# Two transformer blocks on one core: longer runs of small matmuls, another beginning, and a last projection with tokens on the partitions

## The chip, the cores and the metric

The kernel runs on one core of a Trainium2 chip. Its time is the time on the device in microseconds (us). Each core has five engines with instruction lists of their own, worked off in order: TensorE (PE, matmuls into PSUM; PEld is its loading of the stationary operand), VectorE (DVE), ScalarE (ACT), GpSimd (POOL) and SyncE (SP, which here only issues transfers). A list waits where its next instruction needs something that another engine or a transfer has not yet delivered.

## The reference

512 tokens of width 1024 in float32 pass two layers of a first block and one layer of a second. Cut to what matters here:

```
for l in range(2):
    h = rmsnorm(x, attn_norm[l])
    z = h @ w_in[l]            # c_q c_kv k_rope g_q g_k g_v g_lr g_g r_q r_k r_v r_g
    y_a = mla_branch(...)      # softmax attention, 4 heads, low-rank q and kv
    y_b = gla_branch(g_q, g_k, g_v, g_lr, g_g, ...)   # 4 heads, dk 32, dv 64
    y_c = retention_branch(r_q, r_k, r_v, r_g, ...)   # 4 heads, dk 32, dv 64
    x = x + concat([y_a, y_b, y_c]) @ w_out[l]
    h = rmsnorm(x, ffn_norm[l])
    u = h @ ffn_w_up[l]
    x = x + (silu(causal_dwconv(u[..., :2816], ...)) * u[..., 2816:]) @ ffn_w_down[l]
x = rmsnorm(x, final_norm)
# second block: windowed attention, grouped-query attention, attention to a memory
merged = gate_a * (oa @ w_br_a) + gate_b * (ob @ w_br_b) + gate_m * (om @ w_br_m)
out = merged @ w_out
x = x + rms_norm(out, g_post)

# inside gla_branch, a chunk of 64 tokens:
A = einsum('bhik,bhjk,bhijk->bhij', qb, kb, exp(b_i - b_j) for j <= i)
out = A @ v + (q * exp(b)) @ state
# inside retention_branch: scores = (q @ k) * D;  out = scores @ v + q_dec @ R
```

## The kernel before

The class `Prog` issues everything through a framework that tracks what depends on what and sets the order of each engine's list. Activations lie feature-major: x is a tile of 128 partitions x 8 x 512 tokens (`self.x`). Every product with a weight matrix is done as three matmuls with operands split into a high and a low part (`mm3`, L444 to L446: high x high, low x high, high x low), called dense matmuls here. In the profile `ps` is a dense product with the features on PSUM's partitions, `pt` one with the tokens there. A group of weights is loaded by SP (`load`, L407, tile `wst`), its high part taken on ACT (`whi`, L424) and the low part on DVE (`wlo`, L425); up to three groups are staged and three are split at a time.

A dense product is a generator. The queue `Fill` holds such generators, and `self.f(us)` pulls about so many microseconds of dense matmuls from it into the list; the table `PACE` says how many are pulled at each place. So small matmuls of the attention parts and dense ones alternate on PE.

PSUM's eight banks are two tags: three for dense products (`bank`), five for all else (`mbank`).

- **Beginning** (`__init__`, `layer`, `kr_dense`): SP loads x0, the first weight group kr, x1 to x7, and then the groups gqk0 and gqk1 (first and second half of the 1024 features of 256 columns). ACT makes xh and the squares, DVE xl and the sum `acc`. `tsq` (L515) sums over the partitions by transposes, `rsqrt` (L496 to L500) is a chain of tiny DVE steps on `Rt`, and `rows` (L529) spreads the result over the partitions, which ACT copies as R (L539). kr (80 columns) and then gqk run on PE meanwhile; glr, gq, gk are those products times R, and `u` (L781) needs glr.
- **GLA** (`gla`): the causal scores of a chunk are made level by level; at each of eight levels (five of them with masks, MASKED) 16 to 64 matmuls `lv` (L858) of 32 rows fill four banks, one for each head, and DVE (masked copies, L871) or ACT copies them into gD and gA. `f(PACE["gla"])` stands after each quarter of a level (each t).
- **`mix_out`** (L912, for GLA with gA, for retention with rA, twice each in two layers, so four places): for each of four tiles of 128 tokens and each head, two matmuls `o`, one for each half of 64 tokens: the first half with 64 rows of A and v, the second with 128. For t > 0 a matmul with the state (L907) comes first.
- **Retention** (`ret`): per head one bank `rsc` of four matmuls (L968), a product with the decay (`rA`, DVE) and `f(PACE["ret2"])`. Before them `states` (L886) makes U and, on DVE, the states.
- **End** (`finish`): w_out of the second block in four groups of 256 columns, tokens in two halves of 256 moving columns; squares on ACT, sums on DVE, then `tsq`, `rsqrt`, `rows`, product, and the sum with x. Result (1024, 512), which the host transposes.

The functions that the change touches:

## Time and profile before

| | |
|---|---|
| time before, median of 3 runs | 1990.25 us (1987.42 to 1991.47) |
| the profiled execution's own time, and its span | 1990.08 us, 1988.3 us |
| mean granted clock of PE over the span | 0.993 of full speed |
| PE busy | 1954.8 us, 98% |
| DVE busy | 1239.2 us, 62% |
| ACT busy | 793.4 us, 40% |
| POOL busy | 140.7 us, 7% |
| instructions | 28658 |

The span is the profile's stretch from the first to the last instruction on the engines; 1.8 us of the time lie around it. Busy shares are averages over the span. In a row of the trace a matmul of 4-byte numbers may have two records (the loading and the passes split it), so counts of records (x16) are not counts of matmuls; "busy" of a group of records that overlap reaches from the first one's start to the last one's end. The time from the start of one row to the start of the next is what the list spends.

### The profile page before, as it was taken

What the parts mean: (1) busy time and instruction counts of PE and PEld (TensorE: products, weight loads), DVE (VectorE), ACT (ScalarE), POOL (GpSimd) and SP (SyncE); (2) the same over time, 40 slices, a digit from 0 to 9 for tenths busy, and PEclk for the clock granted to TensorE, in tenths of its full rate; (3) what the DMA queues carried; (4) which work ended last, traced back from release to release, by engine and by line L of the source; (5) the groups of instructions that cost most, each with busy time, mean ns of one, the idle gap of its engine ahead of it and who ended that gap; (6) DMA issues with size and microseconds to landing.
All of it is one profiled execution on the core that took longest, in us unless ns stands there. A gap on an engine that the chain in (4) does not pass through costs nothing.

```text
span 1988.3 us, 28658 instructions
## 1 busy us (share of the span) xinstructions
PE 1954.8 (98%) x11351; PEld 1620.4 (81%) x11351; DVE 1239.2 (62%) x2299; ACT 793.4 (40%) x1473; POOL 140.7 (7%) x172
## 2 busy tenths in 40 slices
PE   9999999999999999999999999999999999999997
PEld 7879888888888878888888888887888877788887
DVE  6666576646556666576656466845456787655454
ACT  5545243222224635443222224525354456543242
POOL 1000000000000100000000000021131330000000
PEclk9999999999999999999999999999999999999998
DMA  5221123232323321133232334432222221123331
GB/s 196 60 80 44 64 89 101 84 109 85 106 80 107 94 67 50 41 96 95 93 90 96 103 113 123 135 109 67 75 75 67 75 64 54 63 67 98 101 96 54
DMA packets 55189, 172.30 MB, mean 87 GB/s; under 512 B 6494, under 2 KB 10096, under 8 KB 55056
## 3 DMA queue, kind: packets, MB, share of 16 engines
q1 hardware_dynamic: 53152, 165.47, 26.6%
q0 software_dynamic: 1760, 4.87, 0.9%
q8 instruction: 89, 1.46, 0.3%
q14 instruction: 44, 0.36, 0.1%
q10 hardware_dynamic: 144, 0.14, 0.0%
HBM read 167.05 MB, written 2.10 MB: 85 GB/s over the span
## 4 chain that ended last, share of the span: by engine, by line
PE 91%; DVE 5%; ACT 3%; issue 1%; POOL 0%; DMA 0%; DVEq 0%; POOLq 0%; ACTq 0%
PE ps L444 24%; PE ps L446 23%; PE ps L445 23%; PE pt L444 3%; PE pt L445 3%; PE pt L446 3%; PE o L912 2%; DVE wlo L425 1%; PE o L1029 1%; PE s L1006 1%; PE aq L1347 1%; PE bo L1596 1%; PE bpq L1584 1%; PE rows L529 1%; PE lv L858 1%
## 5 line engine op out<-in xcount | busy, mean ns | idle before, releaser
L424 ACT ACTIVATE whi<-wst 128x1024 fp32r<-128x1024 f32 (+3 forms) x318 | 316.3, 995 | 700.3 <-PE ps L445 566.4
L425 DVE TENSOR_TENSOR wlo<-wst,whi 128x1024 fp32r<-128x1024 f32 (+3 forms) x318 | 367.4, 1155 | 315.9 <-ACT whi L424 315.4
L444 PE MATMUL ps<-xh,whi 128*128 128x512 f32 (+1 forms) x1408 | 556.8, 396 | 0.0
L445 PE MATMUL ps<-xl,whi 128*128 128x512 f32 (+1 forms) x1408 | 550.3, 391 | 0.6 <-DVE xl L490 0.6
L446 PE MATMUL ps<-xh,wlo 128*128 128x512 f32 (+1 forms) x1408 | 549.8, 391 | 0.1
L444 PEld LDWEIGHTS ps<-xh,whi 128*128 128x128 f32 (+1 forms) x1408 | 264.4, 188 | 61.1 <-issue 6.7
L446 PEld LDWEIGHTS ps<-xh,wlo 128*128 128x128 f32 (+1 forms) x1408 | 264.3, 188 | 57.1 <-DVE wlo L425 0.9
L445 PEld LDWEIGHTS ps<-xl,whi 128*128 128x128 f32 (+1 forms) x1408 | 264.6, 188 | 55.8 <-DVE xl L490 2.8
L444 PE MATMUL pt<-whi,xh 128*128 128x256 f32 x480 | 143.2, 299 | 1.5 <-ACT bz L1523 0.8
L445 PE MATMUL pt<-wlo,xh 128*128 128x256 f32 x480 | 137.6, 287 | 0.0
L445 PE MATMUL ps<-fl,whi 128*128 128x512 f32 x352 | 137.0, 389 | 0.0
L444 PE MATMUL ps<-fh,whi 128*128 128x512 f32 x352 | 137.0, 389 | 0.0
L446 PE MATMUL ps<-fh,wlo 128*128 128x512 f32 x352 | 136.9, 389 | 0.0
L446 PE MATMUL pt<-whi,xl 128*128 128x256 f32 x480 | 136.5, 286 | 0.0
L444 PEld LDWEIGHTS pt<-whi,xh 128*128 128x128 f32 x480 | 92.7, 194 | 6.7 <-ACT bz L1523 1.3
L1067 DVE TENSOR_TENSOR x<-x,ps 128x512 f32<-128x512 f32 x96 | 65.7, 687 | 50.8 <-PE ps L446 50.6
L445 PEld LDWEIGHTS pt<-wlo,xh 128*128 128x128 f32 x480 | 93.3, 194 | 0.5 <-issue 0.2
L446 PEld LDWEIGHTS pt<-whi,xl 128*128 128x128 f32 x480 | 92.9, 194 | 0.2 <-issue 0.2
L445 PEld LDWEIGHTS ps<-fl,whi 128*128 128x128 f32 x352 | 66.1, 188 | 13.8
L446 PEld LDWEIGHTS ps<-fh,wlo 128*128 128x128 f32 x352 | 66.1, 188 | 13.7
L444 PEld LDWEIGHTS ps<-fh,whi 128*128 128x128 f32 x352 | 66.1, 188 | 13.6
L486 ACT ACTIVATE fh<-cv 128x512 fp32r<-128x512 f32 x44 | 27.9, 633 | 84.7 <-DVE cv L1121 84.7
(464 smaller groups left out, 2919.1 us busy)
## 6 DMA issues: line engine op xcount, KB each, us to landing
wst<-in_w SPq DMA_DIRECT2D x250, 512.0 KB, 3.5
wst<-in_w SPq DMA_DIRECT2D x54, 384.0 KB, 3.0
wst<-in_w SPq DMA_DIRECT2D x20, 256.0 KB, 2.6
x<-in_xT SPq DMA_DIRECT2D x8, 256.0 KB, 4.9
out<-out SPq DMA_DIRECT2D x8, 256.0 KB, 2.3
mt<-in_memT POOLq DMA_DIRECT2D x4, 256.0 KB, 4.1
c<-in_cst POOLq DMA_DIRECT2D x3, 256.0 KB, 3.5
s<-in_cst POOLq DMA_DIRECT2D x3, 256.0 KB, 2.9
```

The costliest lines, as they stand in the source:

```text
L424: nc.scalar.activation(hi, s3, AF.Copy)
L425: nc.vector.tensor_sub(lo, s3, hi.bitcast(F32))
L444: nc.tensor.matmul(out, lh, rh, start=start, stop=False, skip_group_check=True)
L445: nc.tensor.matmul(out, lh, rl, start=False, stop=False, skip_group_check=True)
L446: nc.tensor.matmul(out, ll, rh, start=False, stop=stop, skip_group_check=True)
L486: nc.scalar.activation(hi, src, AF.Copy)
L529: nc.tensor.matmul(ps[:, t, :], w, self.ident, start=True, stop=True)
L858: nc.tensor.matmul(ps[h][j0:j0 + w, t, c0:c0 + w], ke[hp, a:a + w], qe[hp, a + off:a + off + w], start=True, stop=True, tile_position=(32 ...
L912: nc.tensor.matmul(o[r, j, hd], A[h][:n, t, r], v[t][:n, hd], start=t + h == 0, stop=True, skip_group_check=True)
L1006: nc.tensor.matmul(s[:, :nk], qn[h][:, T4[qt]], kn[h][:, :nk], start=False, stop=True, skip_group_check=True)
L1029: nc.tensor.matmul(O[qt][:, h, :], PT[u][:, T4[kt]], v[kt][:, T4[h]], start=kt == 0, stop=kt == qt)
L1067: nc.vector.tensor_add(xm, xm, ps)
```

## The change

Ten edits go together:

1. x0, x2, x4, x6 are issued by SP and x1, x3, x5, x7 by ACT; the first three weight groups stand on SP after x0, x2 and x4.
2. kr's weights are split in two halves into tiles of their own, and kr and gqk share each part of x: for each of the eight parts three matmuls for kr, then six for gqk.
3. The squares of layer 0's first norm are made by GpSimd; DVE adds them up.
4. In `gla` the dense work of a level is pulled once, after all 32 matmuls, in place of four times.
5. In `mix_out` the state matmuls of a pair of tiles come first, and all A times v have 128 rows.
6. In `ret` all four heads' scores stand in one run, the heads rotating, in four banks.
7. w_out of the second block comes as two groups of 512 columns.
8. `residual` transposes x to token-major (32 transposes, in place) while branch products are worked off.
9. `finish` has the tokens on the partitions: the token tile of x is the stationary operand, 512 columns move; sums of squares come from ACT's accumulator, each tile of 128 tokens has its own small `rsqrt`, and one fused DVE instruction scales and adds x.
10. g_post is loaded as an array of its own by GpSimd, and the result leaves as (512, 1024) in eight transfers, half issued by SP and half by ACT.

```
-    two("out", "w_out_2", k8, _span(0, 1024))
+    for i in range(2):
+        g.append(((2, "out", i), "w_out_2", 0, k8, _span(512 * i, 512)))
...
         for k in range(8):
-            nc.sync.dma_start(self.x[:, k], aps["xT"][128 * k:128 * k + 128])
-            if k == 0:
-                self.load(0)
-        self.load(2)
+            (nc.scalar if k % 2 else nc.sync).dma_start(self.x[:, k], aps["xT"][128 * k:128 * k + 128])
+            if k % 2 == 0:
+                self.load(min(k // 2, 2))
...
+        if i in (self.table[(0, "kr")][0], self.table[(1, "kr")][0]):
+            hi, lo = (TileList([self.gt(n, (128, 4, mc), F32R) for _ in range(2)], 4) for n in ("krwh", "krwl"))
+            for j in range(2):
+                self.split(hi.tiles[j], lo.tiles[j], s3[:, 4 * j:4 * j + 4])
+            self.wt[i] = (k, kt, hi, lo)
+            return
...
-    def sumsq(self, tiles, gain=None):
+    def sumsq(self, tiles, gain=None, pool=False):
         nc = self.nc
         acc = self.gt("acc")
+        if pool:
+            for i, s in enumerate(tiles):
+                q = self.gt("sq") if i else acc
+                nc.gpsimd.tensor_mul(q, s, s)
+                if i:
+                    nc.vector.tensor_add(acc, acc, q)
+            return acc
...
-        ps, pg = {}, {}
-        yield from self.dense((l, "kr"), self.xh, self.xl, 8, ps.__setitem__)
-        yield from self.dense((l, "gqk"), self.xh, self.xl, 8, pg.__setitem__)
+        ps, pg = [self.bank("ps")], [self.bank("ps") for _ in range(2)]
+        _, _, rh, rl = next(self.weights((l, "kr")))
+        for k0, kt, hi, lo in self.weights((l, "gqk")):
+            for k in range(kt):
+                x = self.xh[:, k0 + k], self.xl[:, k0 + k], k0 + k == 0, k0 + k == 7
+                sl = slice(0, 80)
+                self.mm3(ps[0][:80], rh[:, k0 + k, sl], rl[:, k0 + k, sl], *x)
+                yield 0.65
+                for m in range(2):
+                    sl = slice(128 * m, 128 * m + 128)
+                    self.mm3(pg[m], hi[:, k, sl], lo[:, k, sl], *x)
+                yield 1.3
         while self.R is None:
             yield 0.5
...
                         nc.tensor.matmul(ps[h][j0:j0 + w, t, c0:c0 + w], ke[hp, a:a + w], qe[hp, a + off:a + off + w],
                                          start=True, stop=True, tile_position=(32 * h, j0))
-                f(PACE["gla"])
+            f(4 * PACE["gla"])
...
+            first = True
             for j in range(2):
                 t = 2 * tp + j
-                sl = slice(t * 128, t * 128 + 128)
                 if t:
-                    nc.tensor.matmul(o[:, j], qg[:, sl], st[t], start=j == 0, stop=True, skip_group_check=True)
+                    nc.tensor.matmul(o[:, j], qg[:, t * 128:t * 128 + 128], st[t], start=first, stop=True,
+                                     skip_group_check=True)
+                    first = False
+            for j in range(2):
+                t = 2 * tp + j
                 for h in range(4):
                     hd = slice(64 * h, 64 * h + 64)
-                    for n in (64, 128):
-                        r = slice(n - 64, n)
-                        nc.tensor.matmul(o[r, j, hd], A[h][:n, t, r], v[t][:n, hd], start=t + h == 0, stop=True,
+                    for r in (slice(0, 64), slice(64, 128)):
+                        nc.tensor.matmul(o[r, j, hd], A[h][:, t, r], v[t][:, hd], start=False, stop=True,
                                          skip_group_check=True)
...
+        ps = [self.mbank("rsc", (128, 4, 128)) for _ in range(4)]
+        for t in range(4):
+            for h in range(4):
+                hp = slice(32 * h, 32 * h + 32)
+                nc.tensor.matmul(ps[h][:, t, :], rk[hp, T4[t]], rq[hp, T4[t]], start=True, stop=True)
         for h in range(4):
-            hp = slice(32 * h, 32 * h + 32)
-            ps = self.mbank("rsc", (128, 4, 128))
-            for t in range(4):
-                nc.tensor.matmul(ps[:, t, :], rk[hp, T4[t]], rq[hp, T4[t]], start=True, stop=True)
             a = self.gt("rA", (128, 4, 128))
-            nc.vector.tensor_mul(a, ps, rd[:, h:h + 1, :].to_broadcast([128, 4, 128]))
+            nc.vector.tensor_mul(a, ps[h], rd[:, h:h + 1, :].to_broadcast([128, 4, 128]))
             A.append(a)
-            f(PACE["ret2"])
+        f(4 * PACE["ret2"])
...
+            if i == 1:
+                fill.add("res", self.residual())
...
+    def residual(self):
+        nc = self.nc
+        self.xt = self.x.rearrange("p (a b) s -> p a (b s)", b=2).rearrange("p a (t c) -> p a t c", t=4)
+        for kp in range(4):
+            ps = [self.mbank("xT", (128, 2, 2, 128)) for _ in range(2)]
+            for t in range(4):
+                for b in range(2):
+                    nc.tensor.transpose(ps[t // 2][:, t % 2, b], self.x[:, 2 * kp + b, self.T4[t]], self.ident)
+            for j in range(2):
+                nc.scalar.activation(self.xt[:, kp, 2 * j:2 * j + 2], ps[j].rearrange("p t b c -> p t (b c)"), AF.Copy)
+            yield 0.9
...
+        for c in range(2):
+            t = self.gt("gpost")
+            src = self.aps["gpost"]
+            nc.gpsimd.dma_start(t, bass.AP(tensor=src.tensor, offset=src.offset + 512 * c, ap=[[0, 128], [1, 512]]))
+            g.append(t)
...
+        ss = self.small("oss", (4, 2))
+        y = {}
+
+        def ev(t, c, ps):
+            sq = self.gt("osq2")
+            nc.scalar.activation(sq, ps, AF.Square, accum_out=ss[:, t, c:c + 1])
+            y[t, c] = self.gt("oy2")
+            nc.vector.tensor_mul(y[t, c], ps, g[c])
+
+        ps = [self.bank("ps") for _ in range(3)] + [self.mbank("po")]
+        for k0, kt, hi, lo in self.weights((2, "out", 0)):
+            for k in range(kt):
+                for t in range(4):
+                    self.mm3(ps[t], self.xh[:, k0 + k, T4[t]], self.xl[:, k0 + k, T4[t]], hi[k], lo[k],
+                             k0 + k == 0, k0 + k == 7)
+        for t in range(4):
+            ev(t, 0, ps[t])
+        kept = list(self.weights((2, "out", 1)))
+        for t in range(4):
+            ps = self.mbank("po")
+            for k0, kt, hi, lo in kept:
+                for k in range(kt):
+                    self.mm3(ps, self.xh[:, k0 + k, T4[t]], self.xl[:, k0 + k, T4[t]], hi[k], lo[k],
+                             k0 + k == 0, k0 + k == 7)
+            ev(t, 1, ps)
+            v = self.small("ov", (1,))
+            nc.vector.tensor_reduce(v, ss[:, t], AX, OP.add)
...
+            r = self.rsqrt(v, "ort", (1,))
+            for c in (1, 0):
+                o = y[t, c].rearrange("p (a b) -> p a b", a=2)
+                nc.vector.scalar_tensor_tensor(o, o, r, self.xt[:, 2 * c:2 * c + 2, t], op0=OP.mult, op1=OP.add)
+                (nc.sync if c else nc.scalar).dma_start(self.aps["out"][T4[t], 512 * c:512 * c + 512], y[t, c])
```

How this moves instructions is read from the order of the engines' lists. First PE's list in layer 0, at the level of GLA whose matmuls are `lv<-gq,gk` (`pt` and `ps` rows are dense); before:

```order
L858 MATMUL lv<-gq,gk 64x64 x8
L444 MATMUL ps<-cqh,whi 128x512
L445 MATMUL ps<-cql,whi 128x512
L446 MATMUL ps<-cqh,wlo 128x512
L858 MATMUL lv<-gq,gk 64x64 x8
L444 MATMUL ps<-cqh,whi 128x512
L445 MATMUL ps<-cql,whi 128x512
L446 MATMUL ps<-cqh,wlo 128x512
L444 MATMUL ps<-cqh,whi 128x512
L445 MATMUL ps<-cql,whi 128x512
L446 MATMUL ps<-cqh,wlo 128x512
L858 MATMUL lv<-gq,gk 64x64 x8
```

after:

```order
L450 MATMUL ps<-cqh,whi 128x512
L451 MATMUL ps<-cql,whi 128x512
L452 MATMUL ps<-cqh,wlo 128x512
L880 MATMUL lv<-gq,gk 64x64 x32
L450 MATMUL ps<-cqh,whi 128x512
L451 MATMUL ps<-cql,whi 128x512
L452 MATMUL ps<-cqh,wlo 128x512
L450 MATMUL ps<-cqh,whi 128x512
```

The four pieces of 8 have become one run of 32, and the dense rows that stood between them now stand behind it. Four other levels change alike: the 21 pieces of `lv` that these five levels have in a layer become 6 (one level stands in two).

Next PE's list in `mix_out` of layer 0's GLA, second pair of tiles; `gA` is A, `st` a state, before:

```order
L912 MATMUL o<-tv,gA 64x64 x6
L907 MATMUL o<-st,qg 128x256
L912 MATMUL o<-tv,gA 64x64 x6
L444 MATMUL ps<-ckh,whi 128x512
L445 MATMUL ps<-ckl,whi 128x512
L446 MATMUL ps<-ckh,wlo 128x512
L444 MATMUL ps<-ckh,whi 128x512
L445 MATMUL ps<-ckl,whi 128x512
L446 MATMUL ps<-ckh,wlo 128x512
L912 MATMUL o<-tv,gA 64x64
L907 MATMUL o<-st,qg 128x256
L912 MATMUL o<-tv,gA 64x64 x8
```

after:

```order
L929 MATMUL o<-st,qg 128x256
L450 MATMUL ps<-ckh,whi 128x512
L451 MATMUL ps<-ckl,whi 128x512
L452 MATMUL ps<-ckh,wlo 128x512
L450 MATMUL ps<-ckh,whi 128x512
L451 MATMUL ps<-ckl,whi 128x512
L452 MATMUL ps<-ckh,wlo 128x512
L937 MATMUL o<-tv,gA 64x64 x16
L929 MATMUL o<-st,qg 128x256 x2
L937 MATMUL o<-tv,gA 64x64 x3
```

The state matmuls of t = 2 and 3 stand together, ahead of the products with gA, and the products' runs are longer.

Last PE's list at the beginning, where `rows` spreads the first norm; before, 18 dense rows follow until `u`, of which the first two stand here:

```order
L444 MATMUL ps<-xh,whi 128x512
L445 MATMUL ps<-xl,whi 128x512
L446 MATMUL ps<-xh,wlo 128x512
L529 MATMUL rows<-c_ident,Rt 128x128 x4
L444 MATMUL ps<-xh,whi 128x512
L445 MATMUL ps<-xl,whi 128x512
```

after, `u` among the rows:

```order
L452 MATMUL ps<-xh,krwl 80x512
L450 MATMUL ps<-xh,whi 128x512
L451 MATMUL ps<-xl,whi 128x512
L452 MATMUL ps<-xh,wlo 128x512
L450 MATMUL ps<-xh,whi 128x512
L451 MATMUL ps<-xl,whi 128x512
L452 MATMUL ps<-xh,wlo 128x512
L535 MATMUL rows<-c_ident,Rt 128x128 x4
L803 MATMUL u<-wg,glr 128x128 x4
L450 MATMUL ps<-xh,whi 128x512
```

The dense rows that stood between `rows` and `u` now stand ahead of `rows`. On ACT's list the split of the fourth and fifth weight group (`whi`) stands ahead of the copy R, and on DVE's list the adds of the squares stand between the low parts of those groups:

```order
L431 TENSOR_TENSOR wlo<-wst,whi 128x1024
L571 TENSOR_TENSOR acc<-acc,sq 128x512
L431 TENSOR_TENSOR wlo<-wst,whi 128x1024
L571 TENSOR_TENSOR acc<-acc,sq 128x512 x4
L431 TENSOR_TENSOR wlo<-wst,whi 128x1024
L571 TENSOR_TENSOR acc<-acc,sq 128x512
L431 TENSOR_TENSOR wlo<-wst,whi 128x1024
L571 TENSOR_TENSOR acc<-acc,sq 128x512
L523 TENSOR_REDUCE ss<-tsq 128x4
```

Before, the splits of the fourth and fifth group stood behind the last add, in the stretch around `rows`.

## Rows read from the trace of the kernel before

**Rows 1.** The page's sections 1 (busy time by engine) and 4 (chain that ended last).

```profile
PE 1954.8 (98%) x11351; PEld 1620.4 (81%) x11351; DVE 1239.2 (62%) x2299; ACT 793.4 (40%) x1473; POOL 140.7 (7%) x172
PE 91%; DVE 5%; ACT 3%; issue 1%; POOL 0%; DMA 0%; DVEq 0%; POOLq 0%; ACTq 0%
```

**Rows 2.** Windows: stretch, its length, PE, PEld, DVE, ACT, POOL busy, granted clock, DMA.

```profile
83.85:136.76 52.91, 52.40 (x533) 38.31 (x532) 32.64 (x59) 20.00 (x38) 3.13 (x3) 1.00 0.26 76
197.88:222.15 24.27, 24.27 (x199) 19.71 (x197) 12.18 (x25) 7.20 (x12) 0.00 (x0) 1.00 0.14 44
1927.26:1974.85 47.59, 47.34 (x391) 46.75 (x389) 22.11 (x48) 17.71 (x43) 1.30 (x1) 1.00 0.22 68
1974.85:1988.30 13.45, 1.60 (x6) 1.13 (x6) 7.18 (x20) 0.75 (x2) 1.27 (x1) 0.60 0.22 78
0.00:28.32 28.32, 24.25 (x99) 16.97 (x99) 19.74 (x36) 17.31 (x25) 2.54 (x10) 1.00 0.75 252
69.60:73.00 3.40, 3.32 (x15) 3.35 (x16) 2.85 (x4) 2.56 (x5) 0.00 (x0) 0.50 0.02 5
```

**Rows 3.** Timeline of PE, layer 0, GLA: start, busy, instruction, records.

```profile
79.06 0.86 PE L858 MATMUL lv<-qe,ke 32*64 32x64 f32 x58
86.12 0.37 PE L858 MATMUL lv<-qe,ke 32*64 32x64 f32 x16
88.04 0.37 PE L858 MATMUL lv<-qe,ke 32*64 32x64 f32 x16
```

**Rows 4.** Timeline of PE, layer 0, `mix_out` of GLA and dense matmuls behind it.

```profile
127.92 0.70 PE L907 MATMUL o<-st,qg 128*128 128x256 f32 x2
128.55 2.12 PE L912 MATMUL o<-tv,gA 64*64 64x64 f32 x16
131.40 0.40 PE L444 MATMUL pt<-whi,ckh 128*128 128x512 f32 x1
132.09 0.40 PE L444 MATMUL pt<-whi,ckh 128*128 128x512 f32 x1
```

**Rows 5.** Timeline of PE, retention, and windowed attention in the second block.

```profile
199.48 0.54 PE L886 MATMUL U<-tv,rkd 128*32 128x64 f32 x24
202.66 1.71 PE L968 MATMUL rsc<-rT 32*128 32x128 f32 x16
1375.34 0.66 PE L1363 MATMUL ao<-apt,av 128*64 128x128 f32 x8
1375.83 0.61 PE L1363 MATMUL ao<-apt,avo 128*64 128x128 f32 x8
```

**Rows 6.** Timeline of the tail, PE and DVE, with the wait ahead in brackets.

```profile
1975.87 0.41 PE L515 MATMUL tsq<-c_ident,acc 128*128 128x128 f32 x2 [1.02 <-DVE acc L1691]
1976.78 0.17 DVE L1694 TENSOR_SCALAR ss<-ss 128x2 f32<-128x2 f32 x1
1979.06 1.20 PE L529 MATMUL rows<-c_ident,rt 128*128 128x128 f32 x4 [2.78 <-DVE rt L500]
1984.18 0.69 DVE L1701 TENSOR_TENSOR out<-out,x 128x512 f32<-128x512 f32 x1
```

**Rows 7.** Beginning: GB/s in slices of 0.75 us from 0 to 30, then timelines of PE and ACT.

```profile
GB/s 0 0 37 301 402 382 300 348 358 393 391 418 437 410 421 363 365 400 172 86 303 265 273 300 344 377 273 306 142 0 0 0 131 333 235 22 87 213 371 27
18.47 0.60 PE L515 MATMUL tsq<-c_ident,acc 128*128 128x128 f32 x4
22.03 1.16 PE L529 MATMUL rows<-c_ident,Rt 128*128 128x128 f32 x8 [0.20 <-DVE Rt L500]
27.24 1.15 PE L781 MATMUL u<-wg,glr 17*128 17x128 f32 x8
19.58 1.06 ACT L424 ACTIVATE whi<-wst 128x1024 fp32r<-128x1024 f32 x1 [3.69 <-DMA wst<-in_w]
```

**Rows 8.** Timeline of PE, layer 0, the norm of c_q.

```profile
69.68 2.04 PE L529 MATMUL rows<-c_ident,Rqt 128*128 128x128 f32 x8 [1.97 <-DVE Rqt L500]
```

**Rows 9.** Timeline of DVE, layer 0, masked copies of a level of GLA.

```profile
96.61 0.78 DVE L871 COPY_PREDICATED gD<-c_gmask,lv 128x256 f32<-128x256 int32 x2 [0.50 <-PE lv L858]
```

More of the change, by code (lines that the diff above doesn't have):

```diff
@@ L415, in split_weight @@
         s3 = self.staged.pop(i).rearrange("p (k m) -> p k m", k=kt)
+        if i in (self.table[(0, "kr")][0], self.table[(1, "kr")][0]):
[4 more added lines that the diff above has]
+            return
         if i >= self.table[(2, "out", 0)][0]:
-            hi, lo = (TileList([self.gt(n, (128, 2, 256), F32R) for _ in range(2)], 2) for n in ("oh", "ol"))
-            for j in range(2):
-                self.split(hi.tiles[j], lo.tiles[j], s3[:, 2 * j:2 * j + 2])
+            hi, lo = ([self.gt(n, dtype=F32R) for _ in range(kt)] for n in ("oh", "ol"))
+            for j in range(kt):
+                self.split(hi[j], lo[j], s3[:, j])
             self.wt[i] = (k, kt, hi, lo)
@@ L576, in layer @@
             self.prefetch(self.table[(l, "kr")][0] + 1)
-        acc = self.sumsq([self.x[:, k] for k in range(8)])
+        acc = self.sumsq([self.x[:, k] for k in range(8)], pool=l == 0)
         self.z = {}
@@ L1136, in run @@
         if self.stop:
-            nc.sync.dma_start(self.aps["out"].rearrange("(k p) t -> p k t", p=128), self.x)
+            nc.sync.dma_start(self.aps["out"].rearrange("t (k p) -> p k t", p=128), self.x)
             return
@@ L1667, in finish @@
+    def finish(self):
+        nc, T4 = self.nc, self.T4
+        g = []
+        for c in range(2):
[3 more added lines that the diff above has]
+            g.append(t)
         for k in range(8):
             self.split(self.xh[:, k], self.xl[:, k], self.merged[k], 0.5)
-        kept = {}
-        for half in range(2):
-            tk = slice(256 * half, 256 * half + 256)
-            acc = self.gt("acc")[:, :256]
-            out = [self.gt("out", (128, 2, 256)) for _ in range(4)]
-            for i in range(4):
-                if half == 0:
-                    kept[i] = list(self.weights((2, "out", i)))
-                ps = [self.bank("ps", (128, 256)) for _ in range(2)]
-                for k0, kt, hi, lo in kept[i]:
-                    for m in range(2):
-                        sl = slice(m * 128, m * 128 + 128)
-                        for k in range(kt):
-                            self.mm3(ps[m], hi[:, k, sl], lo[:, k, sl], self.xh[:, k0 + k, tk], self.xl[:, k0 + k, tk],
-                                     k0 + k == 0, k0 + k == 7)
-                for m in range(2):
-                    n = 2 * i + m
-                    if n == 0:
-                        nc.scalar.activation(acc, ps[m], AF.Square)
-                    else:
-                        q = self.gt("sq")[:, :256]
-                        nc.scalar.activation(q, ps[m], AF.Square)
-                        nc.vector.tensor_add(acc, acc, q)
-                    nc.scalar.activation(out[i][:, m], ps[m], AF.Copy, scale=self.vec("g_post_2", n))
-            v = self.tok_sums(acc, 1, 2)
-            nc.vector.tensor_scalar(v, v, 1.0 / D, EPS, op0=OP.mult, op1=OP.add)
-            r = self.rsqrt(v, "rt", (2, 1))
-            R = self.rows(r, 2)[:, :256]
-            dst = self.aps["out"].rearrange("(i k p) t -> i p k t", i=4, k=2)
-            for i in range(4):
-                o = out[i]
-                nc.vector.tensor_mul(o, o, R[:, None, :].to_broadcast([128, 2, 256]))
-                (nc.vector if i else nc.gpsimd).tensor_add(o, o, self.x[:, 2 * i:2 * i + 2, tk])
-                nc.sync.dma_start(dst[i][:, :, tk], o)
@@ L1716, in arrays_of @@
     a["qkn"] = np.stack([q, q[sw], k, k[sw]])
+    a["gpost"] = np.ascontiguousarray(inputs["g_post_2"])
     a["mla_out"] = np.ascontiguousarray(inputs["mla_out_norm"])
@@ L1735 @@
         aps[name] = nc.dram_tensor(f"in_{name}", a.shape, F32, kind="ExternalInput").ap()
-    aps["out"] = nc.dram_tensor("out_0", (D, S), F32, kind="ExternalOutput").ap()
+    aps["out"] = nc.dram_tensor("out_0", (S, D), F32, kind="ExternalOutput").ap()
     with tile.TileContext(nc) as tc:
@@ L1739 @@
     r = run_bass_kernel_spmd(nc, [{f"in_{k}": v for k, v in arrays.items()}], core_ids=[0])
-    return np.ascontiguousarray(r.results[0]["out_0"].T)[None]
+    return np.ascontiguousarray(r.results[0]["out_0"])[None]
```

1 line of the change is left out of this document (removed).

## The prediction

> **What bounds the kernel now.** I read the busy table and the chain that ended last first [rows 1]. TensorE (PE) is busy 98% of the span and holds 91% of the chain, against 5% for VectorE (DVE) and 3% for ScalarE (ACT). So PE's in-order list is the kernel: an edit pays what it takes out of that list, and costs what it makes the list wait. The gain must come from the five stretches that the diff touches, and I read those by themselves [rows 2]: GLA with its `mix_out` in layer 0 (52.91 us; layer 1 has the same list), retention with its `mix_out` (24.27), the last projection (47.59), the tail behind it (13.45, PE busy only 1.60) and the beginning (28.32, PE busy 24.25). In the first three PE is busy over 99%: nothing is waited for there, and only fewer or quicker instructions help. The measured sum is made against the profiled execution, 1990.1 us (span 1988.3 and 1.8 around it); the median of the runs is 1990.25, practically the same.
>
> **GLA's scores (two layers).** Before, a level's 32 small matmuls come as four pieces of 8 (16 records each) with 12 dense matmuls between. From one piece to the next is 88.04 - 86.12 = 1.92 us [rows 3]; 12 dense at 47.59/384 = 0.124, or somewhat less, are 1.43 to 1.49, so a piece costs about 0.45. The 58 records that stand together take 0.86 until the last has drained [rows 3], about 0.9 on the list with the way in and out. 0.45 = f + 16r and 0.9 = f + 58r give r = 0.011 a record and f about 0.3 for a piece however small. The whole stretch gives more: of its 52.91 us the 84 dense matmuls of 256 columns take 10.4, the 90 of 512 (0.23 each, below) 20.7 and `mix_out` about 10.8; 11.0 are left for 21 pieces with 288 records, and 11.0 = 21f + 288 x 0.011 is f = 0.37, since entering a 512 wide row costs more. In the program's order the 21 pieces become 6 per layer: 15 x 0.3 to 0.37 = 4.5 to 5.6. The stretch itself is the nearer row: I take **5.5 per layer**. The dense matmuls themselves only move.
>
> **A times v in `mix_out` (four places).** 16 records `o` take 2.12 with the last one's drain (the row at 128.55) [rows 4], about 0.128 each, so 64 records cost 8.2 us; alternate matmuls use 64 and 128 rows of the array, and they run one after another. After, all have 128 rows and alternate only between the two column halves. The nearest rows of that kind are the 24 records of U in 199.96 - 199.48 = 0.48 us [rows 5] (128x32, four column groups, 64 columns moving: 0.08 for four), and `ao` with 128x64 and 128 columns: 0.49 for 8 from 1375.34 to 1375.83 [rows 5], 0.061 each. By U a pair of halves with 64 columns should take some 0.055, 0.028 a record; by `ao`, if loading is what it shows, 0.061. Bounds for the 64 records: 1.8 and 3.9, and 8.2 if the halves do not overlap. The row by shape (rows, moving columns) is U, so I take 1.9: **6.3 per place**. The state matmuls, 0.63 for two records [rows 4], stand together now: 0.2 less per GLA place.
>
> **Retention's scores.** 16 records `rsc` take 1.71 with the drain [rows 5], about 0.1 each, and the 32 of a layer, in three pieces with their ways in and out, 3.8; one head's four matmuls use the same 32 rows. After, four heads rotate over the four row groups into four banks. Eight waves of 0.1 and 0.2 for the way in: 1.1; 1.8 if only two overlap, 3.5 if they stay serial. I take 1.1: **2.7 per layer**. But something is late next: the first A times v now waits for four `rA` products on DVE, and the states' copies and multiply-adds stand ahead of them. One product of 128x512 costs 0.69 as the last add does (at 1984.18) [rows 6], four 2.75; with the state work (one copy and two fused steps for each of four heads, 0.3 each by estimate) about 3.4 before it, 6.2 us from the end of U. PE's work in between (scores, 24 dense, four transposes) is about 5.2. U and four score banks are also all five banks of that tag. A wait of **1.2 per layer** is taken off (0 to 3).
>
> **Sum of the middle.** GLA 2 x (5.5 + 6.3 + 0.2) = 24.0; retention 2 x (6.3 + 2.7 - 1.2) = 15.6. Both shorten the time by 39.6.
>
> **The last projection and the tail.** 384 matmuls of 256 columns in 47.59 become 192 of 512; three dense ones of that width go by in 132.09 - 131.40 = 0.69 [rows 4], 0.23 each, so 43.9: 3.7 saved. In the tail the end of `out` at 1974.85 is followed by squares, sums over the partitions at 1975.87, eleven tiny steps from 1976.78 until 1979.06, the broadcast of the rows, products and adds until 1984.18 + 0.69 = 1984.87 [rows 6], and the transfer: 13.45 in all [rows 2]. After, the token is the partition: no `tsq`, no `rows`, no broadcast. What is left for the last quarter: 0.3 and 0.65 for the square, 0.4 for the sum and scale, 2.0 for ten of the tiny steps (eleven took 2.28), 1.4 for two fused adds, and from the last add's end to the end of the span 1988.3 - 1984.87 = 3.4: 8.2. Saved 5.2. The first three quarters' chains lie below 5.5 us of PE work each. Against it stand 32 new transposes of x: four like them take 0.60 with draining (at 18.47) [rows 7], 0.1 each: 3.2, and eight banks through five with a copy of 0.6 each add about 0.9. Net **-4.8** (-6.5 to -2).
>
> **The beginning.** Here the order shows what the words do not. In place of 18 dense matmuls between `rows` and `u` there are none. Before: `tsq` 18.47, `rows` 22.03, `u` 27.24, the next dense at 28.32 [rows 7]. After, the last two adds of the squares stand on DVE behind the splits of the groups cq0 and cq1; the former's split on ACT began only at 19.58, after a wait for its transfer [rows 7], and the latter's transfer (0.5 MB at the rate below) lands some 1.3 us later. So the last add ends about 24.3, `tsq` 24.5, `rows` (2.9 later for the same tiny steps, 0.7 for the sum) 28.0. Dense work is used up at 27.2. Then `rows` 0.9, the copy R 0.7, glr 0.7, each with PE waiting: `u` at 30.6, next dense 31.7 against 28.32: **+3.4**. After a wait of 1.97 us PE ran at 1.2 GHz once [rows 8], granted clock 0.50 over 69.60 to 73.00 [rows 2]: half of 3.4 is 1.7, and I put half of that in: +0.9. Together **+4.3** (-2 to +7). The squares on GpSimd take nothing from this, they end by about 22.
>
> The two queues for x: the stretch of the first 28 us shows 0.75 of the DMA engines busy and 252 GB/s on average [rows 2], and from 3 us the slices hold 300 to 437 GB/s [rows 7]; x, kr and two gqk groups are some 3.7 MB, and 3.7 MB at 0.38 MB/us land at about 12 however they are issued. The Trainium skill ("DMA: Bandwidth & Descriptors", section on issuing engines) says the same against this part: queues of different engines share the same 16 DMA engines, so a second one saves only issue time. By that rule the part gives 0 and the sum stands; if the queues did add bandwidth, up to twice the rate, all of it would land by 7 or 8 and the beginning would be worth -2.
>
> **Not seen in any row.** New waits at joined places (bank releases, A ready about 1 us before it is used in GLA): 0 to 6, I put **+2.0**. Sum: -39.6 - 4.8 + 4.3 + 2.0 = -38.1, so 1990.1 - 38.1 = **1952 us**.
>
> **Rivals.**
> A. *The halves of A times v do not overlap.* For: `o` is serial in every row of before [rows 4]. Against: U and `ao` overlap column groups [rows 5]. Price: 4 x 6.3 = 25 us not gained: 1977. With 0.061 a record only 8 are lost: 1960. Chance of the first 0.10, of the second within the next.
> B. *The masks become the bound.* A joined level needs four banks at once out of five; a pair of masked copies takes 0.78 on DVE [rows 9], four 1.6, and they stand in line with other DVE work: DVE is busy 32.64 us of a stretch that shrinks from 52.91 to about 41 [rows 2]. For: 80% busy. Against: 21 to 48 dense matmuls (5 us) stand between levels. If each of the 10 joined levels waits 1.0, 10 come back: 1962. The Trainium skill ("TensorEngine Tiling (Array Packing)", PSUM bottleneck) gives the rule behind this: a quicker TensorE leaves the emptying of PSUM as the limit. No row of before shows it. Chance with A's second case 0.17.
> C. *The beginning does what it says* (data sooner, PE fed): -2 in place of +4.3, and no unseen waits: 1944. Chance 0.10.
> D. *Slower than before.* One mechanism: at every joined place PE waits about 2 us as at 69.68 [rows 8], and each time the clock falls to 1.2 GHz for a stretch as then: 1.97 + 1.7 = 3.7 each. There are about 18 such places (10 levels, 4 + 4 at the two halves of A times v): 67 us, 2019. It decides from 11 places on (11 x 3.7 = 41). Against: in before PE waits over 1 us at only a few places. Chance 0.03.
>
> The forecast has 0.58 with its own range 1945 to 1959. The rest, 0.02, is no change: the joined runs' gain eaten by all of A and B. Reaching to B and C and most of the way to A the range is 1942 to 1972. Measurement can tell about 0.2% (4 us) from no change. Faster 0.95, same 0.02, slower 0.03.
>
> **What would show it.** Right: `o` at about 0.03 a record and some 2 us per place; `rsc` one run of about 1.1; a GLA stretch near 41 us and a retention stretch near 16, PE over 97% busy in both; `u` at 30 or later with PE waiting on R; a tail of about 8 us; 32 transposes in about 4. Wrong: `o` still at 0.1 or more (A); PE waits named after gD or gA in the levels (B); a granted clock below 1.00 in the stretches of GLA or retention (D); x landed by 8 us and `u` before 28 (C).

## The result, and the profile after

The changed kernel takes 1960.49 us (median of 4 runs, 1958.48 to 1969.05), the kernel before 1989.45 (4 runs, 1987.42 to 1991.47): a ratio of 0.9863, 95% interval 0.9832 to 0.9894. The forecast was 1952 in a range of 1942 to 1972, with 0.58 on a band of its own of 1945 to 1959, which the time missed by 1.5. The profiled execution took 1960.82, its span 1959.0.

The page's busy table and its chain, which answer to [rows 1]:

```profile
PE 1915.2 (98%) x11179; PEld 1590.6 (81%) x11179; DVE 1240.4 (63%) x2313; ACT 785.2 (40%) x1459; POOL 152.2 (8%) x180
PE 88%; DVE 6%; ACT 3%; issue 1%; DMA 1%; POOL 0%; DVEq 0%; ACTq 0%; POOLq 0%
```

PE lost 39.6 us of work, but the time fell by 29.3 only: PE is idle for 43.8 us of the span where it was idle for 33.5, and DVE and DMA hold more of the chain. Where, the stretches tell. Windows of after (columns as in [rows 2]; the first five rows answer to its GLA, retention, last projection, tail and beginning; the last is a piece of the first):

```profile
89.67:135.28 45.61, 42.15 (x534) 34.76 (x533) 31.87 (x59) 20.13 (x38) 5.03 (x3) 0.96 0.27 78
196.64:213.09 16.45, 15.16 (x200) 13.24 (x198) 12.34 (x28) 6.96 (x12) 0.00 (x0) 1.00 0.10 33
1906.70:1950.53 43.83, 43.83 (x193) 35.66 (x191) 24.03 (x65) 11.46 (x27) 0.00 (x0) 1.00 0.21 74
1950.53:1959.00 8.47, 0.00 (x0) 0.00 (x0) 3.91 (x15) 0.69 (x2) 0.00 (x0) 0.69 0.31 119
0.00:34.01 34.01, 24.24 (x100) 16.54 (x100) 26.16 (x37) 13.65 (x18) 12.18 (x18) 1.00 0.69 229
124.44:127.26 2.82, 2.82 (x6) 1.78 (x6) 1.60 (x2) 0.09 (x2) 2.15 (x1) 0.50 0.12 16
```

Retention is 7.82 shorter (24.27 to 16.45), the projection 3.76, the tail 4.98. GLA is shorter by only 7.3, and in it PE is idle for 3.46 us; behind that the granted clock is 0.50, the lower of its two levels (1.2 GHz). PE's timeline in the rebuilt runs (start, busy, instruction, records; it answers to [rows 3 to 6]) shows that the runs themselves are as quick as hoped:

```profile
111.12 0.91 PE L880 MATMUL lv<-gq,gk 32*64 32x64 f32 x64
200.16 1.17 PE L993 MATMUL rsc<-rT 32*128 32x128 f32 x32
204.09 0.66 PE L1082 MATMUL yt<-c_ident,on 128*128 128x128 f32 x4 [1.13 <-DVE st L915]
206.92 1.15 PE L937 MATMUL o<-tv,rA 128*64 128x64 f32 x32
1870.55 3.66 PE L1700 MATMUL xT<-c_ident,x 128*128 128x128 f32 x32
```

Less the last one's drain (the next row starts so much later), 32 records `o` take 1.08 us, 0.034 each against 0.128 before; 32 `rsc` 1.10; the 32 new transposes 3.41.

**The new waits.** PE's waits of after that are new or have grown most (engine, line, releaser: us in all, times, longest); `xl` stood at 0.6 before and the other three not at all:

```profile
PE ps L450 <- DVE rt L790: 6.9, 2, 3.4
PE ps L451 <- DVE xl L496: 4.0, 6, 1.0
PE yt L1082 <- DVE st L915: 2.3, 2, 1.1
PE u L803 <- DVE glr L629: 1.5, 1, 1.5
```

`xl` and `u` belong to the beginning, `yt` to retention. For `rt` it is one wait of 3.4 in each GLA layer. The timeline of all engines around it in layer 0 shows a chain over four queues:

```profile
118.50 1.22 DVE L431 TENSOR_TENSOR wlo<-wst,whi 128x1024 fp32r<-128x1024 f32 x1
118.55 2.32 POOL L794 TENSOR_TENSOR qt<-rt,sw 128x512 f32<-128x512 f32 x1 [36.84 <-ACT whi L430]
120.90 1.28 ACT L783 ACTIVATE qr<-qt 64x512 fp32r<-64x512 f32 x2 [2.43 <-POOL qt L794]
121.56 1.41 DVE L784 TENSOR_TENSOR qr<-qt,qr 64x512 fp32r<-64x512 f32 x2 [1.84 <-ACT qr L783]
123.61 0.68 DVE L790 TENSOR_TENSOR rt<-ps,c 128x512 f32<-128x512 f32 x1
124.44 0.76 PE L450 MATMUL ps<-ckh,whi 128*128 128x512 f32 x1 [3.43 <-DVE rt L790]
```

The rope of q's first bank ends in a sum on GpSimd. `stack` then copies it on ACT and subtracts on DVE, and both wait in their queues. The second bank's rope (L790), which empties the PSUM bank that PE wants next, stands on DVE behind that subtraction. Before, the same chain ran:

```profile
114.88 1.28 POOL L772 TENSOR_TENSOR qt<-rt,sw 128x512 f32<-128x512 f32 x1 [38.98 <-DVE sw L769]
117.53 1.40 DVE L762 TENSOR_TENSOR qr<-qt,qr 64x512 fp32r<-64x512 f32 x2
119.58 0.68 DVE L768 TENSOR_TENSOR rt<-ps,c 128x512 f32<-128x512 f32 x1
```

From GpSimd's sum to the second rope it took 4.70 us before and 5.06 in after. But PE spent 5.02 on the 12 dense matmuls and the small ones ahead of that bank (115.52 to 120.54), and came to it 0.28 after the rope had ended. In after, with the small ones joined and moved away, it gets there in 3.45 and has to wait.

**The beginning.** DVE's splits of x by tile, and the timeline of GpSimd, DVE and PE (answers to [rows 7]):

```profile
L496 DVE SCALAR_TENSOR_TENSOR xl<-x,vec,xh x8: 737/1524/1562, 6.7 to 16.5; 128x512 fp32r<-128x512 f32 x8
```

```profile
10.03 5.38 POOL L569 TENSOR_TENSOR sq<-x 128x512 f32<-128x512 f32 x4 [0.43 <-DMA x<-in_xT]
30.29 1.16 PE L535 MATMUL rows<-c_ident,Rt 128*128 128x128 f32 x8 [0.67 <-DVE Rt L506]
32.93 1.15 PE L803 MATMUL u<-wg,glr 17*128 17x128 f32 x8 [1.48 <-DVE glr L629]
```

`u` starts 5.69 us later than before. The minimum, median and maximum of a split are 737, 1524 and 1562 ns: most take twice the shortest while GpSimd squares.

**The account.** The start of the same instruction in both traces, after less before: `u` +5.69; the norm of c_k +5.82 (after has half clock behind `u`, before had it in the row at 69.60 of [rows 2]; they cancel); end of GLA -1.48, start of retention's stretch -1.24, its end -9.07; in layer 1 -8.99, -16.65 (end of GLA), -16.42 and -24.25; end -29.3. So the beginning costs 5.8, GLA gives 7.3 and 7.7, retention 7.8 twice, the end 5.1, and 0.24 is lost between GLA and retention in each layer.

### The profile page after: what moved, and what is told of

Read it like the earlier page. It is cut to its first block, busy times and chain, and to the rows that moved or that the text cites. A ratio compares the mean times of both kernels' runs of the same rounds, so it can differ in the third digit from the quotient of the medians.

```text
span 1959.0 us, 28293 instructions
## 1 busy us (share of the span) xinstructions
PE 1915.2 (98%) x11179; PEld 1590.6 (81%) x11179; DVE 1240.4 (63%) x2313; ACT 785.2 (40%) x1459; POOL 152.2 (8%) x180
## 4 chain that ended last, share of the span: by engine, by line
PE 88%; DVE 6%; ACT 3%; issue 1%; DMA 1%; POOL 0%; DVEq 0%; ACTq 0%; POOLq 0%
PE ps L450 23%; PE ps L451 23%; PE ps L452 23%; PE pt L450 3%; PE pt L452 3%; PE pt L451 3%; DVE wlo L431 1%; PE o L1055 1%; PE s L1032 1%; PE aq L1375 1%; PE bo L1624 1%; PE bpq L1612 1%; ACT whi L430 1%; PE rows L535 1%; DMA x<-in_xT 1%
## 5 line engine op out<-in xcount | busy, mean ns | idle before, releaser
L430 ACT ACTIVATE whi<-wst 128x1024 fp32r<-128x1024 f32 (+2 forms) x316 | 314.3, 995 | 686.6 <-PE ps L451 562.3
L431 DVE TENSOR_TENSOR wlo<-wst,whi 128x1024 fp32r<-128x1024 f32 (+2 forms) x316 | 365.2, 1156 | 333.3 <-ACT whi L430 332.9
L450 PE MATMUL ps<-xh,whi 128*128 128x512 f32 x1392 | 550.7, 396 | 0.1
L451 PE MATMUL ps<-xl,whi 128*128 128x512 f32 x1392 | 544.1, 391 | 0.0
L452 PE MATMUL ps<-xh,wlo 128*128 128x512 f32 x1392 | 543.9, 391 | 0.0
L450 PEld LDWEIGHTS ps<-xh,whi 128*128 128x128 f32 x1392 | 262.2, 188 | 60.6 <-issue 6.7
L452 PEld LDWEIGHTS ps<-xh,wlo 128*128 128x128 f32 x1392 | 262.1, 188 | 55.5
L451 PEld LDWEIGHTS ps<-xl,whi 128*128 128x128 f32 x1392 | 262.4, 189 | 52.6 <-issue 0.2
L1136 POOL MEMSET apad<- 128x2 f32 x44 | 4.3, 101 | 745.6 <-DVE cv L1143 745.6
```

Of the source, the lines that this page charges most:

```text
L430: nc.scalar.activation(hi, s3, AF.Copy)
L431: nc.vector.tensor_sub(lo, s3, hi.bitcast(F32))
L450: nc.tensor.matmul(out, lh, rh, start=start, stop=False, skip_group_check=True)
L451: nc.tensor.matmul(out, lh, rl, start=False, stop=False, skip_group_check=True)
L452: nc.tensor.matmul(out, ll, rh, start=False, stop=stop, skip_group_check=True)
```

## The experiments

Theory 1: the joined runs are cheap, and in GLA the wait behind `stack` gives most of their gain back. Theory 2: the beginning costs because the last squares come late, and the squares on GpSimd slow DVE's splits. The rivals were a slower A times v, a shortage of banks, and the second queue. Each experiment is the changed kernel with one part of it altered, the last one with two. All but the last ran once, and after's own four runs spread over 10 us, so the readings rest on the stretches of the traces and the times only go with them.

**Squares on ACT again.**

```diff
-        acc = self.sumsq([self.x[:, k] for k in range(8)], pool=l == 0)
+        acc = self.sumsq([self.x[:, k] for k in range(8)])
```

> The changed kernel with one edit undone: the eight squares of the first norm are made on ACT again, nothing on GpSimd. In the changed kernel the eight low parts xl took 1.44 us each on DVE (0.75 alone) while GpSimd squared, and u began at 32.93. Theory 1 (GpSimd and DVE exclude each other while both read two operands from SBUF): xl falls back to about 0.7 each, PE no longer waits 0.5 to 1.0 us per part for xl, the sum of squares ends 2 to 3 us earlier and u begins at 30 to 31. Rival 1 (xl is late because x lands late, and its length in the trace is only waiting): xl keeps its pace and u stays at 32.9, or comes later because ACT has 5 us more to do.

The splits by tile, and PE's `u`:

```profile
L496 DVE SCALAR_TENSOR_TENSOR xl<-x,vec,xh x8: 743/744/751, 6.4 to 13.5; 128x512 fp32r<-128x512 f32 x8
30.32 0.93 PE L803 MATMUL u<-wg,glr 17*128 17x128 f32 x6 [1.97 <-DVE glr L629]
```

Every split takes 0.74 and `u` starts 2.61 sooner, 0.3 from the forecast's 30.6. The Trainium skill ("SBUF — State Buffer", section "Who interferes with whom") says that GpSimd shares DVE's second pair of SBUF ports under an exclusive lock. The trace agrees: 0.744 alone, 1.524 beside the squares; and GpSimd's sum `qt` took 2.32 above beside a DVE split (1.28 before). The whole run took 1962.14: the 2.6 and more are there until the second block, where a stretch at half clock (below) took 6 back.

**One queue for x.**

```diff
-            (nc.scalar if k % 2 else nc.sync).dma_start(self.x[:, k], ...
+            nc.sync.dma_start(self.x[:, k], ...
```

> The changed kernel with all eight parts of x issued by SyncE, the weight groups at the same places. Theory (the transfers share one rate of about 0.4 MB per us, whoever issues them): the last part of x lands within 0.7 us of where it lands now, u begins within 0.7 us of 32.93. Rival (a second queue adds rate): the last part lands 2 us or more later, and u too.

1959.03; `u` at 33.09 against 32.93, the last part of x landed at 12.92 against 12.38. The second queue is worth at most 0.2.

**The beginning as before**, the rest of the change kept (both edits above, x also ahead of the second and third weight group, kr's weights undivided, and):

```diff
+        ps, pg = {}, {}
+        yield from self.dense((l, "kr"), self.xh, self.xl, 8, ps.__setitem__)
+        yield from self.dense((l, "gqk"), self.xh, self.xl, 8, pg.__setitem__)
-        for k0, kt, hi, lo in self.weights((l, "gqk")):
...
```

> The changed kernel with the whole beginning as before: x by SyncE ahead of the second and third weight group, kr first and gqk behind it, squares on ACT. Theory (the new beginning costs what u shows, 5.7 us, and the stretch at half clock behind it some 1.5): u begins at 27.2 as before, and everything behind is 5.5 to 7.5 us earlier, the span about 1952 to 1954. Rival (the delay is made up later, since weights are then waiting): u at 27.2 but the span within 2 us of 1959.

1954.40, span 1952.6. `u` starts at 27.23, as in before and 5.70 sooner than in after; the landmarks of the first block come 4.6 to 6.3 sooner. The new beginning is a loss of some 6.

**Both ropes read before either is stacked.**

```diff
-            self.rope64(t, ps, CR, SR)
-            self.stack(qr[2 * m:2 * m + 2], t)
+            self.rope64(ts[m], ps, CR, SR)
+            if m:
+                for j in range(2):
+                    self.stack(qr[2 * j:2 * j + 2], ts[j])
```

> The changed kernel with one change of order: the two halves of the roped queries in MLA are both read out of PSUM (rope) before either is split for stacking; no work is added or taken away. In the changed kernel PE waits 3.43 us in each layer for a PSUM bank that the second rope on DVE frees, and this rope stands behind a subtraction that waits for GpSimd's sum and a copy on ACT; behind the wait PE runs 2.9 us at the lower clock. Theory (that queueing is the wait): PE's wait goes from 3.4 to under 1 us in both layers, the granted clock stays at 1.00 there, and the time falls by 2 x (3.4 + 1.5) = 8 to 10 us, to about 1950 to 1952. Rival (the joined levels leave DVE too busy, whatever the order): the wait moves to another DVE instruction and the time stays within 3 us.

1959.58. The theory fell: the wait does not go, it moves to the next bank that DVE empties behind the subtractions (`kn`, L775), and the time stays; from PE's waits of this kernel:

```profile
PE ps L450 <- DVE kn L775: 6.6, 2, 3.3
```

**The subtraction on GpSimd** (the copy stays on ACT):

```diff
-            nc.vector.tensor_sub(t[b], src[a], t[a].bitcast(F32))
+            (sub or nc.vector).tensor_sub(t[b], src[a], t[a].bitcast(F32))
...
+            self.stack(qr[2 * m:2 * m + 2], t, nc.gpsimd)
```

> The changed kernel with the subtraction that splits the roped queries of MLA (four of 64x512 in a layer) made by GpSimd instead of DVE. In the changed kernel, and with the order changed, PE waited 3.3 to 3.4 us in each layer for a PSUM bank whose emptying stood on DVE behind these subtractions, which wait for GpSimd's sum and ACT's copy. Theory (DVE's in-order list, held by an instruction that waits for others, is the whole wait): DVE no longer waits there, PE's wait falls below 1 us in both layers, no stretch at half clock follows, and the time falls by 8 to 10 us, to 1950 to 1952. Rival (DVE's work in the shortened stretch is simply too much, 80% busy): PE waits over 2 us again, for another DVE instruction.

1963.21, and again the wait moved, to `kn` (two of up to 3.1). The timeline shows why DVE's queue alone was not the cause:

```profile
122.27 1.28 ACT L783 ACTIVATE qr<-qt 64x512 fp32r<-64x512 f32 x2 [2.44 <-POOL qt L794]
124.79 1.06 ACT L430 ACTIVATE whi<-wst 128x1024 fp32r<-128x1024 f32 x1
125.88 2.16 DVE L431 TENSOR_TENSOR wlo<-wst,whi 128x1024 fp32r<-128x1024 f32 x1 [2.92 <-ACT whi L430]
```

ACT's queue is held 2.44 us by the copy that waits for GpSimd. The next weight's `whi` stands behind it, DVE's `wlo` waits 2.92 for `whi`, and the `kn` product stands behind `wlo`. The edit also has a price of its own: this `wlo` took 2.16 beside the subtraction that now ran on GpSimd, the one in after 1.22. My theory that DVE's list alone holds the bank fell.

**`stack` written behind the `kn` products**, in the next generator:

```diff
-            self.stack(qr[2 * m:2 * m + 2], t)
+            z.setdefault("qt", []).append(t)
...
+        for m, t in enumerate(z.pop("qt")):
+            self.stack(z["qr"][2 * m:2 * m + 2], t)
```

> The changed kernel with the splitting of the roped queries (a copy on ACT, a subtraction on DVE, four of each in a layer) written behind the emptying of the four kn banks; same work, same engines. With the subtraction on GpSimd the wait only moved: DVE then stood at a low part wlo behind a high part that ACT makes behind its own copy, which waits for GpSimd's sum. Theory (whatever instruction waits for GpSimd's sum, on DVE or on ACT, holds the emptying of PSUM behind it; nothing is too slow in itself): with no such instruction ahead, PE's wait for rt or kn falls below 1 us in both layers, no half clock follows, and the two GLA stretches are 4 to 5 us shorter each: 1950 to 1952. Rival (DVE's and ACT's sheer work in the shortened stretch bounds it): PE still waits over 2 us there.

1954.59, above the forecast's 1950 to 1952. The waits named `rt` and `kn` are gone from PE's list; the window of its GLA stretch:

```profile
89.69:129.99 40.30, 40.25 (x533) 33.74 (x532) 31.53 (x59) 19.93 (x38) 3.94 (x3) 1.00 0.34 99
```

40.3 is the prediction's 41, with PE busy throughout and DVE 78%. At the end of the first block the kernel stands 12.7 ahead of after (-36.92 against -24.25), but the whole gained 5.9. The rest is in the combine of the second block, whose program is the same in both; windows at equal times, where this kernel is 12.7 us further on, first this kernel, then after:

```profile
1545.00:1560.00 15.00, 13.50 (x35) 7.80 (x35) 8.87 (x21) 2.69 (x4) 7.69 (x6) 0.58 0.10 35
1560.00:1575.00 15.00, 15.00 (x32) 9.66 (x33) 10.54 (x11) 3.36 (x5) 8.01 (x7) 0.51 0.12 35
```

```profile
1545.00:1560.00 15.00, 12.80 (x66) 10.06 (x65) 12.68 (x45) 5.83 (x13) 4.08 (x4) 1.00 0.25 78
1560.00:1575.00 15.00, 15.00 (x59) 9.32 (x58) 12.46 (x19) 5.80 (x9) 11.56 (x9) 1.00 0.07 29
```

At clock 0.5 half as many records of matmuls go by, 67 against 125. In both kernels PE has just waited 2.13 us for `cf` (at 1546.50 here, at 1559.19 in after); behind it the clock fell here and stayed down for some 27 us, and in after it did not fall. Half of 27 is not lost in full: after waits 3.9 us for `bs` further on (the row `PE bs L1599 <- DVE bqT L784: 3.9, 1, 3.9` of its waits) and has some 7 us of half clock behind that, this kernel neither. Against after and before about 6 is lost, as in the run with the squares on ACT. No edit touches this stretch.

**GLA's levels in quarters again**, the rest of the change kept:

```diff
-            f(4 * PACE["gla"])
+                f(PACE["gla"])
```

> The changed kernel with the joined levels of GLA undone: dense work is pulled after each quarter of a level again. Theory 1 (what saved in the levels is given back by the new wait, which comes from the shortening of the whole stretch): 15 pieces of 0.37 come back, 5.5 us per layer, and the wait of 3.4 with its half clock of 1.5 shrinks or goes, so that the time stays within 3 us of 1960. Theory 2 (the wait comes from the shorter products A times v alone, behind the levels): the wait stays as it is and the time grows by about 11 us, to 1971.

1960.12, the same as after. The stretch:

```profile
89.71:136.72 47.01, 46.40 (x533) 34.78 (x532) 32.45 (x59) 19.86 (x38) 3.13 (x3) 1.00 0.25 77
```

No wait over 0.4 and full clock, as Theory 1 has it. So joining the levels is worth 47.01 - 40.30 = 6.7 in the stretch of GLA where nothing waits, and 47.01 - 45.61 = 1.4 in the change as it was made (layer 0; 0.4 in layer 1). A part of the 6.7 goes back further on: with the levels in quarters retention takes 15.70 in place of 16.45, without the wait ahead of `yt`, and the way to it 0.23 less.

**A times v: both halves of a head apart**, **row counts alternating again**, and **retention's heads in turn**:

```diff
-                for h in range(4):
-                    hd = slice(64 * h, 64 * h + 64)
-                    for r in (slice(0, 64), slice(64, 128)):
+                for r in (slice(0, 64), slice(64, 128)):
+                    for h in range(4):
+                        hd = slice(64 * h, 64 * h + 64)
```

> The changed kernel with the A times v matmuls of a tile in another order: first all heads' first half of 64 tokens, then all heads' second half, all with 128 rows as in the change; nothing added or left out. Theory (two column halves overlap when they alternate): without alternating a record takes about 0.1 us again instead of 0.034, and 32 records of rA some 3.5 us instead of 1.08. Rival (what cost time before was the change between 64 and 128 rows, and the constant shape alone makes it quick): 32 records stay at 1.1 to 1.3 us.

```diff
-                        nc.tensor.matmul(o[r, j, hd], A[h][:, t, r], v[t][:, hd], ...
+                        nc.tensor.matmul(o[r, j, hd], A[h][:n, t, r], v[t][:n, hd], ...
```

> The changed kernel with only the row counts of A times v undone: the first half of 64 tokens uses 64 rows of A and v again, the second 128; the state matmuls stay ahead. Theory (a change of the row count keeps neighbours from overlapping): a record takes 0.128 us as before the change, 32 records some 4.1 us, and the four places give back 4 x 6 = 24 us less what then hides the new waits in GLA (about 8): 1975 to 1985. Rival (alternating halves is enough, the row count does not matter): 32 records stay near 1.1 us and the time at 1960.

```diff
-        for t in range(4):
-            for h in range(4):
+        for h in range(4):
+            for t in range(4):
```

> The changed kernel with the scores of retention in one run and four banks, but head by head, so that four neighbours use the same 32 rows. Theory (row groups overlap when neighbours use different ones): 32 records take 3.4 to 3.6 us instead of 1.10, in each layer, and since the wait for the products behind them starts later too, the time grows by 4 to 5 us. Rival (the one run is what saves, by its fewer ways in and out): 32 records stay below 1.5 us.

The three runs as PE's timeline of each kernel has them:

```profile
209.04 1.54 PE L937 MATMUL o<-tv,rA 128*64 128x64 f32 x32
```

```profile
218.04 4.18 PE L938 MATMUL o<-tv,rA 64*64 64x64 f32 x32
```

```profile
200.16 2.82 PE L993 MATMUL rsc<-rT 32*128 32x128 f32 x32
```

Up to the next row the 32 records `o` take 1.47 with the halves apart (0.046 each) and 4.1 with the row counts alternating (0.128), against 1.08 (0.034). So 0.082 of the 0.094 gained a record stay when only the row count is constant, and my theory that the alternation of the halves makes the gain mostly fell: it is worth 0.4 in 32. The halves still overlap in part there: single records of one half start 0.058 apart, and the next half begins before the last is through. Without any overlap 0.070 of the 0.094 would be left, by estimate from that spacing. The Trainium skill ("TensorEngine Tiling (Array Packing)", "Key Properties") says that changing the tiling mode, not the tile within it, drains the engine; these three prices agree. The first of these kernels took 1970.05 (about 6 of it again half clock in the combine), the second 1994.60, 34 more than after and above its forecast of 1975 to 1985: the runs cost 24 of it by themselves (8 of 32 records, 3.0 each), and the waits of 3.4 are not hidden by them, they stand there as in after (6.9 in two). The other 10 agree with the clock: from the end of the wait in layer 0 on it was 0.51 (123.98 to 141.05, PE busy 16.54 of 17.07), and over the span its mean was 0.987 against 0.993, which is 12 us of full clock. Why it stayed down longer there is open.

Retention's heads in turn take 2.75, in rotation 1.10, and the kernel's time is the same (1960.85, forecast 4 to 5 more): `yt`, ahead of which PE waited 1.13 for DVE, starts only 0.37 later, and retention ends within 0.01. Against the 3.8 of the forecast's working, joining alone gave 1.05; the rotation's 1.65 fall into that wait.

**The old beginning and the late `stack` together:**

> The changed kernel with the beginning of before (x by one queue ahead of the second and third group, kr ahead of gqk, squares on ACT) and with the splitting of the roped queries behind the kn banks. If the two costs are independent, 6.2 and 8 to 10 us come off: 1944 to 1947, a ratio to before of 0.977 to 0.979. If the wait in GLA does not go with the later splitting, 1952 to 1955.

1941.92 us (median of 5 runs, 1941.17 to 1943.35) against 1989.86 (9 runs): ratio 0.9760, 95% interval 0.9746 to 0.9774. It beats both kernels, and by 2 us the forecast: against after the beginning gives about 6, the two GLA stretches 5.3 and 6.3, and 1.5 comes from half clock between `u` and GLA in layer 1 that after has and this kernel has not; the combine lost nothing more. Its GLA stretch:

```profile
83.66:123.97 40.31, 40.27 (x533) 33.72 (x532) 31.50 (x59) 19.92 (x38) 3.96 (x3) 1.00 0.31 99
```

## Why the prediction was right, and where its sum was off

- **Direction and place: right.** PE's list was the bound, and the time fell where it got shorter. The rebuilt runs measured: `o` 0.034 a record (forecast 0.03), the stretch of GLA 40.3 without the wait (41), retention -7.82 a layer (-7.8), the projection 43.83 (43.9; the forecast's own 192 x 0.23 is 44.2), the tail 8.47 (8.2), transposes 3.41 (4.1), the whole end -5.1 (-4.8).
- **The range held partly by luck.** 1960.49 lies outside the forecast's own band, at the prices of A's second case (1960) and of B (1962), and neither happened. Two signs of being right failed with it: GLA's stretch was 45.61 and not near 41, and PE was busy 92% of it and of retention's, not over 97%. One sign of being wrong came, that of D: a granted clock of 0.96 in GLA.
- **"Not seen in any row: +2.0" was mis-sized.** It measured 11.5: the late `stack` shortens GLA against after by 5.3 in layer 0 and 6.2 in layer 1. That is a wait of 3.4 on the bank behind `stack` in each, and clock lost behind it. In layer 0 it gave back 5.3 of the 6.7 that joining the levels is worth. The rows for it were in the trace of before: four queues that wait for one another with a GpSimd sum in the middle. I priced PE's list and counted only DVE's busy share, which at 78% bounds nothing even now.
- **"The squares on GpSimd take nothing from this" failed.** They take 2.6 us, through DVE's splits. Without them `u` starts at 30.32; the forecast says 30.6, though its terms (28.0 + 0.9 + 0.7 + 0.7) add up to 30.3. The beginning measured +5.8 against +4.3; of the 0.9 for a lower clock nothing is left in the account, since before lost about as much at 69.60.
- **A times v: right in size, in part for another reason.** The forecast took its price from U, where neighbours overlap in different column groups. Most of what was gained comes from the constant row count; the alternation of the halves gives 0.012 of 0.094 a record.
- **Retention's wait of 1.2 for DVE** came to its size but not at its place: PE waits 1.13 ahead of `yt`, for the state steps on DVE that read U's bank (U and the four score banks are all five, as the forecast remarks), and only 0.15 for `rA`.
- **The rivals.** A fell: `o` is not serial at constant rows. B fell in its mechanism: no level waits for its masks. Its price came by another way. C fell: x landed at 12.4, as forecast (about 12), and `u` started at 32.93. D's mechanism, a wait with a halved clock behind it, is what happened, at 2 places and not 11, and not at the joined runs but at the bank behind `stack`.
- In the forecast's terms the measured sum is -26.6 (GLA without the new wait, 12.6 and 14.0; forecast -24.0), +11.5 (the new wait, +2.0), -15.6 (retention, -15.6), -5.1 (end, -4.8), +5.8 (beginning, +4.3) and +0.6 in between: -29.4, within rounding of the 29.3 measured, where the forecast had -38.1.

Left open: why the clock stays down in the combine in some executions. It stayed at half for some 27 us behind the wait for `cf` in the single executions of three kernels (squares on ACT, halves apart, late `stack`), and for at most some 10 us in all the other traces. It may be part of why after's runs spread over 10 us: the one of 1969.05 had a mean granted clock of 0.986, the other three 0.993 to 0.996. Where in that run the clock was low no trace shows.

## What to carry to other kernels

When PE's list is shortened, look at what its old length covered: follow each PSUM bank back over all queues that empty it, and move the writing of whatever waits for a slow engine (here GpSimd) behind the instructions that empty banks. Of small matmuls, keep the row count constant and stand them together; rotating row groups pays only where no other engine is late next. Don't put work on GpSimd beside DVE instructions with two SBUF inputs that stand on the path.

## What the runs showed of the hardware that was not expected

- A DVE instruction with two SBUF inputs (128x512) took 1.52 us in place of 0.74 beside GpSimd's squares, and a GpSimd sum 2.32 in place of 1.28 beside a DVE split.
- In the combine the granted clock was 0.58 and 0.51 over two stretches of 15 us in which PE was busy 13.50 and 15.00 (the late `stack`); in after it was 1.00 with 12.80 and 15.00, and the wait ahead was 2.13 us in both. So here the clock did not follow PE's busy time alone, and it stayed at 0.51 through 15 us in which PE was busy throughout.
- Alternating 64 and 128 rows costs about 0.08 to 0.09 us at every record of a matmul of 64 columns (0.128 against 0.034 to 0.046), and each of these matmuls has two records.
